# The state-space part with channels on partitions: decay and norm factors by DMA broadcast, skip and norm weights per partition

## The chip, the cores and the metric

One of the cores of a Trainium2 chip runs the whole kernel in one launch. The metric is device time in microseconds (us). TensorE (PE in the profile) multiplies matrices, PEld are its weight loads, VectorE is DVE, ScalarE ACT, GpSimd POOL, SyncE SP. All data is float32; most products are done as three products of rounded parts (hi x hi, hi x lo, lo x hi).

## What is computed

A decoder layer on 1024 positions of 1024 features: an input projection, two branches (a Conformer convolution of 31 taps and a Mamba-2 state-space branch), gates, an output projection and a gated MLP with layer norms. The change concerns the state-space branch. Cut to that (32 heads of 64 channels, 4 groups of 8 heads, state size 128, chunks of 128 positions):

```python
xbc = silu(causal_dwconv(xbc, conv_w, conv_b))          # x, B, C
dt = softplus(dt_raw + dt_bias);  a = dt * -exp(a_log)
a_cs = cumsum(a)                                        # inside a chunk
decay = where(causal, exp(a_cs[l] - a_cs[s]), 0)
y_diag = einsum(cb * decay, x * dt)                     # cb = C B^T, per chunk
states = einsum(B, exp(a_cs[-1] - a_cs), x * dt)        # carried from chunk to chunk
y_off  = einsum(C, prev_state) * exp(a_cs)
y = y_diag + y_off + x * d_skip
yg = y * silu(z);  yg = yg * rsqrt(mean(yg**2 over the 512 channels of a group) + eps)
return (yg * norm_w) @ w_out
```

## The kernel before, in words

The sequence is done in two halves of 512 positions. `mixers(hh)` holds the input projection and both branches of a half: for each of the four groups it projects the columns of B, C and the four x tiles and convolves them with 4 taps (`conv4`, L418 to L432), projects z (`z_gate`), projects two tiles of the Conformer's GLU (`glu`), and does the state-space part (`ssd_group`) in four chunks of 128 positions. The Conformer's 31 taps (`conv31`, L467) are recorded at lower priority and fill VectorE. A scheduler that models the engines' times sets the order of instructions on each engine; the order is fixed when the program is built, and each engine works through its own list. So the products of the next group's columns, z and GLU stand between the chunks of a group.

A projection is 24 products of 512 columns (L183 to L185) into one of four PSUM banks (`acc`); its weights are loaded by SyncE, copied rounded by ScalarE (L159), and the remainder is made by VectorE (L160). Small products use four other banks (`sm`).

A chunk of `ssd_group`: x tiles are transposed so that positions lie on partitions (L519), GpSimd prepares the exponents (`au`, L525), TensorE and ScalarE make the decay mask `m` (L534, L542, L543), VectorE multiplies it with C B^T (L559). Eight products of `m` with 64 columns of `xs` each give the inner part with positions on partitions and channels in columns (`py`, L581); one product of 512 columns gives the state's part (`po`, L562), scaled by VectorE with `edc` per position. VectorE adds the skip (L551), the state's part (L567) and `py` (L582) and multiplies with the chunk's z tile (L583), ScalarE squares with a row sum (L585). `normed` takes the root (L588) and reciprocal (L589) of the four chunks' sums, scales the four tiles (L591, with the norm weights as a broadcast row `nw`), and transposes them to channels on partitions for the output projection:

```python
A.activation(out=ssq, in_=ssq, func=AF.Sqrt, bias=eps, scale=1.0 / HALF)
V.reciprocal(out=ssq, in_=ssq)
for c in range(4):
    V.scalar_tensor_tensor(out=ts[c], in0=ts[c], scalar=ssq[:, c : c + 1], in1=nw, ...)
    transpose_to(yT, ts[c], c, (g % 2) * 4, 4)
```

z tiles come from a pool of five buffers (`zs`), each [128 positions, 512 channels]. Its four banks are filled side by side, and the four activations (L495) follow. The first output projection (`ssm_out_first`, weights `w_so`) reads the tiles of groups 0 and 1 in the time of group 2; the second (`w_sp`, in `combine`, L658) those of groups 2 and 3, right after the gate columns (`w_gt`, `w_gb`).

Of the kernel before, what the change touches and what calls it, by code (L numbers as in the profile page):

```python
# [8 lines left out]
F32 = mybir.dt.float32  # L9
# [36 lines left out]
RW_NW = 6 * D  # L46
RW_AL = RW_NW + 2 * D
RW_SD = RW_AL + HEADS
RW_N = RW_SD + HEADS

# [6 lines left out]
def kernel(  # L57
# [71 lines left out]
    dskip = statep.tile([P, HEADS], F32, name="dskip")  # L129
# [8 lines left out]
    edc = statep.tile([P, 3, 4, HEADS], F32, name="edc")  # L138
# [12 lines left out]
    g_scr = [dram.tile([8, P, HALF], F32, name=f"g_scr{i}") for i in range(2)]  # L151
    y_scr = [dram.tile([8, P, HALF], F32, name=f"y_scr{i}") for i in range(2)]
# [111 lines left out]
    def ln_in(hh):  # L264
        hT = big_tile(f"hT{hh}")
        with pool(f"lnin{hh}", side="right") as pl:
# [12 lines left out]
            if first:  # L279
                SY.dma_start(pc[:, :PC_N], pcol)  # L280
                SY.dma_start(a_log, prow[RW_AL : RW_AL + HEADS].partition_broadcast(P))
                SY.dma_start(dskip, prow[RW_SD : RW_SD + HEADS].partition_broadcast(P))
# [12 lines left out]
    def time_steps(pl, hh, ps):  # L295

        n2 = 2 * HEADS
        dtc = pl.tile([n2, HALF], F32, tag="yo", name=f"dtc{hh}")
# [48 lines left out]
        for c in range(4):  # L347
# [6 lines left out]
            )  # L354
        hi = pl.tile([P, HALF], F32R, tag="xsd", name=f"sp_hi{hh}")
# [18 lines left out]
        for i, m in enumerate((upper, later, ones)):  # L374
            TE.matmul(pe[:, i * n : (i + 1) * n], m, a, start=True, stop=True)
        ev = edc.rearrange("p i c h -> p (i c h)")
        A.activation(out=ev, in_=pe[:, : 3 * n], func=AF.Exp)
        V.tensor_mul(wds, dtv, edc[:, 1].rearrange("p c h -> p (c h)"))
# [99 lines left out]
    def z_gate(pl, hh, hT, g):  # L478

        pss = [bank(1) for _ in range(4)]  # L480
        for kp in range(4):
            w = weights(wz[g, kp], f"z{hh}_{g}_{kp}")
            for t in range(4):
                for k in range(2):
                    mm3(
                        pss[t],
                        lambda i: hT[:, i, 2 * kp + k, t * P : (t + 1) * P],
                        lambda i: w[:, i, k * HALF : (k + 1) * HALF],
                        kp == 0 and k == 0,
                        kp == 3 and k == 1,  # L490
                    )
        zs = []
        for t in range(4):
            z = pl.tile([P, HALF], F32, tag="zs", bufs=5, name=f"zs{hh}_{g}_{t}")
            A.activation(out=z, in_=pss[t], func=AF.Silu)  # L495
# [821 lines left out]
```

## Time and profile before

| | us |
|---|---|
| median of 3 runs (1996.41 to 1998.56) | 1997.97 |
| profiled execution | 1997.83 |
| its span | 1995.9 |
| PE busy | 1963.0 (98%) |
| DVE busy | 1688.2 (85%) |
| ACT busy | 1025.6 (51%) |
| POOL busy | 170.2 (9%) |
| granted TensorE clock, mean | 0.998 |

A group's row gives line, engine, operation, output and inputs by the program's names, shapes, the count, then the busy time in us and the mean of one in ns, then the idle time in front of it and what ended it. A row of the timeline begins with its start from the span's start and its duration, both in us; xN are N instructions in one row, the duration then from the first's start to the last's end.

### The profile page before, as it was taken

Reading aid. Unit: us, or ns where it says so; the run is one execution under the profiler, and the core shown is the slowest. Engines: PE = TensorE matmul, PEld = TensorE weight load, DVE = VectorE, ACT = ScalarE, POOL = GpSimd, SP = SyncE. Lnnn points to the kernel's source line nnn. Section 1 sums busy time; section 2 is a strip of 40 time slices with the busy share of each in tenths; the row PEclk is TensorE's granted clock in tenths of the full one; section 3 lists DMA queues with packets and bytes.
Section 4 is the critical chain, followed back from the end, with each engine's and each line's share of the span. In section 5 each row is a group of like instructions: output and inputs, shape, how many; then the busy total and the mean of one; then the engine's idle time right before and its main releaser. Section 6 shows DMA issues by size and latency. Waiting matters only on the chain. (4 is left out here: it accounts for less than half of the span.)

```text
span 1995.9 us, 24560 instructions
## 1 busy us (share of the span) xinstructions
PE 1963.0 (98%) x9140; PEld 1619.0 (81%) x9140; DVE 1688.2 (85%) x2257; ACT 1025.6 (51%) x1490; POOL 170.2 (9%) x143
## 2 busy tenths in 40 slices
PE   7999999999999999999999999999999999999997
PEld 6888887888788888888888888887878888888886
DVE  7599999989865868999998987578998888788868
ACT  5465654556453265665545546255555544553432
POOL 1010101001310000100000122001000000011000
PEclk9999999999999999999999999999999999999999
DMA  6213223333445632222323243477443232368572
GB/s 223 95 64 96 80 89 107 96 111 102 168 136 164 229 124 74 85 90 85 116 90 111 101 166 125 137 277 250 154 155 110 100 122 95 106 225 270 181 242 106
DMA packets 97032, 272.21 MB, mean 136 GB/s; under 512 B 11216, under 2 KB 11216, under 8 KB 96912
## 3 DMA queue, kind: packets, MB, share of 16 engines
q1 hardware_dynamic: 88992, 246.78, 36.8%
q0 software_dynamic: 5616, 19.66, 2.7%
q10 hardware_dynamic: 2304, 4.20, 0.6%
q8 instruction: 72, 1.18, 0.2%
q14 instruction: 48, 0.39, 0.1%
HBM read 221.05 MB, written 49.55 MB: 136 GB/s over the span
## 5 line engine op out<-in xcount | busy, mean ns | idle before, releaser
L467 DVE SCALAR_TENSOR_TENSOR c<-v,pc,c 128x512 f32<-128x512 f32 x480 | 374.5, 803 | 7.1 <-ACT c L456 5.6
L525 POOL TENSOR_TENSOR au<-seg_mv,head_of 128x1024 fp32r<-128x1024 f32 x32 | 74.8, 2336 | 958.6 <-PE sm L534 728.7
L183 PE MATMUL acc<-hT,w_c 128*128 128x512 f32 x352 | 140.9, 400 | 0.0
L184 PE MATMUL acc<-hT,w_c 128*128 128x512 f32 x352 | 140.6, 399 | 0.0
L185 PE MATMUL acc<-hT,w_c 128*128 128x512 f32 x352 | 138.5, 394 | 0.0
L956 DVE SCALAR_TENSOR_TENSOR fo<-u,pc,fo 128x1024 f32<-128x1024 f32 x88 | 111.3, 1284 | 0.4 <-ACT fo L952 0.4
L422 DVE SCALAR_TENSOR_TENSOR xbc<-u,pc,xbc 128x512 f32<-128x512 f32 x144 | 109.6, 773 | 0.5 <-ACT xbc L420 0.4
L183 PE MATMUL acc<-h1s,w_s 128*128 128x512 f32 x264 | 103.4, 392 | 2.3 <-ACT u L940 2.3
L185 PE MATMUL acc<-h1s,w_s 128*128 128x512 f32 x264 | 103.0, 390 | 0.0
L184 PE MATMUL acc<-h1s,w_s 128*128 128x512 f32 x264 | 102.8, 389 | 0.0
L184 PE MATMUL acc<-w_z,hT 128*128 128x512 f32 x256 | 100.9, 394 | 0.0
L183 PE MATMUL acc<-w_z,hT 128*128 128x512 f32 x256 | 100.7, 400 | 0.0
L185 PE MATMUL acc<-w_z,hT 128*128 128x512 f32 x256 | 100.6, 396 | 0.0
L159 ACT CAST w_c<-st_c 128x1024 fp32r<-128x1024 f32 x48 | 50.4, 1051 | 91.8 <-PE acc L185 67.5
L1095 ACT CAST w_dn<-dr 128x1024 fp32r<-128x1024 f32 (+1 forms) x73 | 60.9, 843 | 67.9 <-DVE dr L1025 35.0
L1096 DVE TENSOR_TENSOR w_dn<-dr,w_dn 128x1024 fp32r<-128x1024 f32 (+1 forms) x73 | 70.2, 967 | 14.7 <-ACT w_dn L1095 14.5
L184 PEld LDWEIGHTS acc<-hT,w_c 128*128 128x128 f32 x352 | 66.1, 188 | 16.8 <-issue 3.9
L185 PEld LDWEIGHTS acc<-hT,w_c 128*128 128x128 f32 x352 | 66.1, 188 | 16.1 <-issue 2.6
L183 PEld LDWEIGHTS acc<-hT,w_c 128*128 128x128 f32 x352 | 66.1, 188 | 15.9 <-issue 2.6
L160 DVE TENSOR_TENSOR w_c<-st_c,w_c 128x1024 fp32r<-128x1024 f32 x46 | 59.3, 1288 | 16.7 <-ACT w_c L159 16.7
L183 PE MATMUL sm<-h1b,w_s 128*128 128x512 f32 x176 | 69.1, 393 | 0.0
L184 PE MATMUL sm<-h1b,w_s 128*128 128x512 f32 x176 | 69.0, 392 | 0.0
(366 smaller groups left out, 5698.0 us busy)
## 6 DMA issues: line engine op xcount, KB each, us to landing
st_c<-wcol SPq DMA_DIRECT2D x50, 512.0 KB, 3.5
st_z<-wz SPq DMA_DIRECT2D x32, 512.0 KB, 3.4
st_wo<-wo SPq DMA_DIRECT2D x24, 512.0 KB, 4.2
ra<-wup SPq DMA_DIRECT2D x22, 512.0 KB, 3.5
rb<-wup SPq DMA_DIRECT2D x22, 512.0 KB, 3.4
t_scr<-fo POOLq DMA_DIRECT2D x22, 512.0 KB, 3.4
dr<-t_scr SPq DMA_DIRECT2D x44, 256.0 KB, 4.0
dr<-wdown SPq DMA_DIRECT2D x38, 256.0 KB, 4.3
```

The costliest lines, as they stand in the source:

```text
L159: A.copy(w[:, 0, :], st)
L160: (eng or V).tensor_tensor(out=w[:, 1, :], in0=st, in1=w[:, 0, :].bitcast(F32), op=ALU.subtract)
L183: TE.matmul(ps, wa(0), xa(0), start=start, stop=False, skip_group_check=more)
L184: TE.matmul(ps, wa(0), xa(1), start=False, stop=False, skip_group_check=more)
L185: TE.matmul(ps, wa(1), xa(0), start=False, stop=stop, skip_group_check=more)
L422: V.scalar_tensor_tensor(out=o, in0=u[:, k : k + HALF], scalar=pc[:, wc + k : wc + k + 1], in1=o, op0=ALU.mult, op1=ALU.add,)
L467: V.scalar_tensor_tensor(out=accs[i], in0=v[:, k : k + HALF], scalar=pc[:, wc + k : wc + k + 1], in1=accs[i], op0=ALU.mult, op1=ALU.add,)
L525: G.tensor_tensor(out=au, in0=seg_mv[:, c, :].unsqueeze(1).to_broadcast([P, 8, P]), in1=head_of[:, g, :].unsqueeze(2).to_broadcast([P, 8, P]),
L956: V.scalar_tensor_tensor(out=o, in0=u[:, k : k + T], scalar=pc[:, wc + k : wc + k + 1], in1=o, op0=ALU.mult, op1=ALU.add,)
L1095: A.copy(w[:, 0, cs], src)
L1096: V.tensor_tensor(out=w[:, 1, cs], in0=src, in1=w[:, 0, cs].bitcast(F32), op=ALU.subtract)
```

## The change

The state-space part leaves its result with channels on partitions.

- `z_gate` projects z like every other column, with weights as the stationary operand, so that a z tile is [128 channels, 512 positions].
- In a chunk `py` has `xs` (64 channels wide) as stationary operand and `m` as moving one, so that a head's result goes to 64 partitions, even heads to the lower, odd heads to the upper half (L577 now). The state's part is four products of 128 columns with slices of the state as the stationary operand (L563 now).
- All four chunks write into one tile `acc` [128, 4, 512]. It is preloaded with the decay factors exp(a_cs): they are made per half on ScalarE, written to memory (`e_scr`) and read back per group by two DMAs of GpSimd's queue that repeat a head's row on its 64 partitions. A chunk multiplies its part of `acc` with `po` and adds `py` (L564, L587 now).
- After the fourth chunk, tile by tile: the x tile, scaled by a weight per partition, plus `acc` (L591 now), times z (L595 now), in place in the x tile; squares on ScalarE, their sum over the four tiles on GpSimd (`ss`, L597 to L601 now).
- `normed` sums the squares over partitions with four products (`pick`, L606 now), takes root and reciprocal on [4, 128] values, writes them to memory (`r_scr`) and reads them back as a row on all partitions (L614, L615 now), both on GpSimd's queue; scales the x tiles (L618 now) and splits them with `split_to` (L203, L204 now). The 16 transposes per group are gone.
- The weights for skip and norm come as columns (`nskip`), no longer as rows.

The order of instructions changes with it. A name's first number is the half, the second the group, the third the chunk or tile; the last number only counts buffers. Order on ScalarE around the end of group 1 in the first half, before; `zs0_2` are the z tiles of group 2, `acc` their banks, `sq` the squares:

```order
L495 ACT_TABLE_LOAD
L495 ACTIVATE zs0_2_0_2433<-acc109_2313 128x512
L495 ACTIVATE zs0_2_1_2435<-acc110_2314 128x512
L495 ACTIVATE zs0_2_2_2437<-acc111_2315 128x512
L542 ACTIVATE m0_1_3_1931<-sm95_1936 128x512
L585 ACTIVATE sq0_1_2_1919,ssq0_1_1770<-t0_1_2_1892 128x512
L543 ACT_TABLE_LOAD
L543 ACTIVATE m0_1_3_1931<-m0_1_3_1931 128x512
L159 CAST w_ga0_5_2511<-st_ga0_5_2509 128x1024
L495 ACT_TABLE_LOAD
L495 ACTIVATE zs0_2_3_2439<-acc112_2316 128x512
```

And there now:

```order
L163 CAST w_gg0_5_2532<-st_gg0_5_2530 128x1024
L597 ACTIVATE ss0_1_1958<-xbc0_4_1381 128x512
L492 ACT_TABLE_LOAD
L492 ACTIVATE zs0_2_1_2367<-acc104_2337 128x512
L600 ACTIVATE sq0_1_1_1964<-xbc0_5_1421 128x512
L492 ACTIVATE zs0_2_2_2399<-acc105_2369 128x512
L600 ACTIVATE sq0_1_2_1969<-xbc0_6_1461 128x512
L492 ACTIVATE zs0_2_3_2431<-acc106_2401 128x512
```

Three of the four z activations of group 2 have moved from the middle of group 1's last chunks to behind group 1's squares; tile 0 still stands earlier. The bank of `acc104` is next used by `acc108`, the first `w_gg` product of that stretch.

VectorE at the same place, before; `c` are the Conformer's taps, `t0_1_3` the fourth chunk of group 1:

```order
L160 TENSOR_TENSOR w_gg0_5_2540<-st_gg0_5_2538,w_gg0_5_2540 128x1024
L467 SCALAR_TENSOR_TENSOR c0_2_2007<-v0_2_1696,pc_114,c0_2_2007 128x512
L467 SCALAR_TENSOR_TENSOR c0_3_2009<-v0_3_1762,pc_114,c0_3_2009 128x512
L582 TENSOR_TENSOR t0_1_3_1944<-t0_1_3_1944,sm98_1960 128x512
L467 SCALAR_TENSOR_TENSOR c0_2_2007<-v0_2_1696,pc_114,c0_2_2007 128x512
L467 SCALAR_TENSOR_TENSOR c0_3_2009<-v0_3_1762,pc_114,c0_3_2009 128x512
L583 TENSOR_TENSOR t0_1_3_1944<-t0_1_3_1944,zs0_1_3_1634 128x512
```

And there now; `xbc0_4` to `xbc0_7` are the x tiles of group 1:

```order
L587 TENSOR_TENSOR ys0_1_1770<-ys0_1_1770,sm95_1948 128x4x128
L474 SCALAR_TENSOR_TENSOR c0_2_1999<-v0_2_1698,pc_114,c0_2_1999 128x512
L474 SCALAR_TENSOR_TENSOR c0_3_2001<-v0_3_1764,pc_114,c0_3_2001 128x512
L591 SCALAR_TENSOR_TENSOR xbc0_4_1381<-xbc0_4_1381,nskip_116,ys0_1_1770 128x512
L591 SCALAR_TENSOR_TENSOR xbc0_5_1421<-xbc0_5_1421,nskip_116,ys0_1_1770 128x512
L591 SCALAR_TENSOR_TENSOR xbc0_6_1461<-xbc0_6_1461,nskip_116,ys0_1_1770 128x512
L591 SCALAR_TENSOR_TENSOR xbc0_7_1501<-xbc0_7_1501,nskip_116,ys0_1_1770 128x512
L474 SCALAR_TENSOR_TENSOR c0_2_1999<-v0_2_1698,pc_114,c0_2_1999 128x512
L474 SCALAR_TENSOR_TENSOR c0_3_2001<-v0_3_1764,pc_114,c0_3_2001 128x512
L164 TENSOR_TENSOR w_gg0_5_2532<-st_gg0_5_2530,w_gg0_5_2532 128x1024
L595 TENSOR_TENSOR xbc0_4_1381<-xbc0_4_1381,zs0_1_0_1540 128x512
```

The first multiplication with a z tile of the group has moved behind the addition of the fourth chunk, the four skips, four taps and a weight remainder. On TensorE, 11 rows (L187 to L189) stand now between the last L577 of group 1 and the first product into `acc108`; at the same place of group 0 they are 32, and in the second half 23 and 7.

VectorE at the norm of group 3 in the first half, before:

```order
L589 RECIPROCAL ssq0_3_3645<-ssq0_3_3645 128x4
L467 SCALAR_TENSOR_TENSOR c0_7_3884<-v0_7_3637,pc_114,c0_7_3884 128x512
L591 SCALAR_TENSOR_TENSOR t0_3_0_3669<-t0_3_0_3669,ssq0_3_3645,nw0_3_3643 128x512
L591 SCALAR_TENSOR_TENSOR t0_3_1_3715<-t0_3_1_3715,ssq0_3_3645,nw0_3_3643 128x512
L591 SCALAR_TENSOR_TENSOR t0_3_2_3767<-t0_3_2_3767,ssq0_3_3645,nw0_3_3643 128x512
L591 SCALAR_TENSOR_TENSOR t0_3_3_3819<-t0_3_3_3819,ssq0_3_3645,nw0_3_3643 128x512
```

And there now:

```order
L612 RECIPROCAL rr0_3_3837<-rr0_3_3837 4x128
L164 TENSOR_TENSOR w_gb0_3_4357<-st_gb0_3_4355,w_gb0_3_4357 128x1024
L618 SCALAR_TENSOR_TENSOR xbc0_12_3236<-xbc0_12_3236,nskip_116,ss0_3_3813 128x512
L618 SCALAR_TENSOR_TENSOR xbc0_13_3276<-xbc0_13_3276,nskip_116,ss0_3_3813 128x512
L618 SCALAR_TENSOR_TENSOR xbc0_14_3316<-xbc0_14_3316,nskip_116,ss0_3_3813 128x512
L618 SCALAR_TENSOR_TENSOR xbc0_15_3356<-xbc0_15_3356,nskip_116,ss0_3_3813 128x512
L204 TENSOR_TENSOR yT0_2_3036<-xbc0_12_3236,yT0_2_3036 128x512
```

One weight remainder stands between reciprocal and scaling, and the DMAs to memory and back lie between them too. On TensorE 72 rows stand between the last L577 of group 3 and its `pick`, and 7 behind it before the first `w_sp` product that reads the new tiles; in the second half likewise.

The diff, cut to its core:

```diff
+        for i in range(4):
+            ps = bank(1)
+            project(ps, weights(wz[4 * g + i], f"z{hh}_{g}_{i}"), hT)
+            z = pl.tile([P, HALF], F32, tag="zs", bufs=5, name=f"zs{hh}_{g}_{i}")
+            A.activation(out=z, in_=ps, func=AF.Silu)
...
+        eh = pl.tile([P, HALF], F32, tag="yo", bufs=2, name=f"sp_eh{hh}")
+        A.activation(out=eh, in_=pa, func=AF.Exp)
+        G.dma_start(e_scr[hh], eh)
...
-        nw = row(pl, RW_NW + g * HALF, HALF, f"nw{hh}_{g}", tag="nw")
+        acc = pl.tile([P, 4, HALF], F32, tag="ys", name=f"ys{hh}_{g}")
+        ev = e_scr[hh].rearrange("(g k i j) t -> g k j i t", k=4, j=2, i=4)
+        for j in range(2):
+            G.dma_start(acc[j * HP : (j + 1) * HP], ev[g, 0, j].partition_broadcast(HP))
...
-            V.tensor_tensor(out=heads(t), in0=heads(px), in1=per_head(dskip[:, h8]), op=ALU.mult)
...
-                TE.matmul(po, CT[:, cs], S, start=True, stop=True)
-                V.tensor_tensor(out=heads(yo), in0=heads(po), in1=per_head(edc[:, 0, c, h8]), op=ALU.mult)
-                V.tensor_add(t, t, yo)
+                for i in range(4):
+                    ts = slice(i * P, (i + 1) * P)
+                    TE.matmul(po[:, ts], S[:, ts], CT[:, cs], start=True, stop=True)
+                V.tensor_tensor(out=acc[:, :, cs], in0=by_tile(po), in1=acc[:, :, cs], op=ALU.mult)
...
-                TE.matmul(py[:, hs], m[:, h, :], xs[:, hs], start=True, stop=True)
-            V.tensor_add(t, t, py)
-            V.tensor_mul(t, t, zs[c])
-            A.activation(out=sq, in_=t, func=AF.Square, accum_out=ssq[:, c : c + 1])
+                TE.matmul(
+                    py[h % 2 * HP : (h % 2 + 1) * HP, h // 2 * P : (h // 2 + 1) * P],
+                    xs[:, h * HP : (h + 1) * HP], m[:, h, :], start=True, stop=True)
+            if first:
+                A.copy(acc[:, :, cs], by_tile(py))
+            else:
+                V.tensor_tensor(out=acc[:, :, cs], in0=acc[:, :, cs], in1=by_tile(py), op=ALU.add)
+        for i, y in enumerate(xT):
+            V.scalar_tensor_tensor(out=y, in0=y, scalar=nskip[:, 1, k : k + 1], in1=acc[:, i, :],
+                op0=ALU.mult, op1=ALU.add)
+            V.tensor_mul(y, y, zs[i])
+            A.activation(out=sq, in_=y, func=AF.Square)
+            G.tensor_add(ss, ss, sq)
...
+            for c in range(4):
+                TE.matmul(pm[:4, :P], pick[:, c, :], ss[:, c * P : (c + 1) * P], start=c == 0, stop=c == 3)
+            A.activation(out=r, in_=pm[:4, :P], func=AF.Sqrt, bias=eps[:4], scale=1.0 / HALF)
+            V.reciprocal(out=r, in_=r)
+            G.dma_start(rd.rearrange("(c t) -> c t", c=4), r)
+            G.dma_start(ss, rd.partition_broadcast(P))
+            for i, y in enumerate(xT):
-                transpose_to(yT, ts[c], c, (g % 2) * 4, 4)
+                V.scalar_tensor_tensor(out=y, in0=y, scalar=nskip[:, 0, k : k + 1], in1=ss,
+                    op0=ALU.mult, op1=ALU.mult)
+                split_to(yT, (g % 2) * 4 + i, y)
```

More of the change, by code (lines that the diff above doesn't have):

```diff
@@ L297, in time_steps @@
         n2 = 2 * HEADS
[L298 removed]
+        dtc = pl.tile([n2, HALF], F32, tag="yo", bufs=2, name=f"dtc{hh}")
         A.activation(
@@ L587, in normed @@
         def normed(yT):
-            A.activation(out=ssq, in_=ssq, func=AF.Sqrt, bias=eps, scale=1.0 / HALF)
-            V.reciprocal(out=ssq, in_=ssq)
+            pm = bank(0)
             for c in range(4):
+                TE.matmul(
+                    pm[:4, :P], pick[:, c, :], ss[:, c * P : (c + 1) * P],
+                    start=c == 0, stop=c == 3,
+                )
+            r = pl.tile([4, P], F32, tag="rr", name=f"rr{hh}_{g}")
+            A.activation(out=r, in_=pm[:4, :P], func=AF.Sqrt, bias=eps[:4], scale=1.0 / HALF)
```

80 lines of the change are left out of this document (39 added, 41 removed).

## The prediction

> **What bounds the kernel now.** I read the page's first part, then the waits of TensorE, then the windows by stage, and last the groups and the timeline around the places that the change touches.
>
> ```profile
> span 1995.9 us, 24560 instructions
> ## 1 busy us (share of the span) xinstructions
> PE 1963.0 (98%) x9140; PEld 1619.0 (81%) x9140; DVE 1688.2 (85%) x2257; ACT 1025.6 (51%) x1490; POOL 170.2 (9%) x143
> ...
> PE sm L209 <- DVE x L260: 13.3, 2, 12.1
> ...
> PE acc L184 <- DVE yT L216: 1.5, 1, 1.5
> ...
> PE acc L183 <- ACT gb L644: 0.6, 1, 0.6
> ```
>
> TensorE is busy in 98% of the span, and its waits (total, times, longest) are the start (13.3 us, before the first transposes) and little else: the two waits for the state-space output in front of `w_sp` are 1.5 and 0.6 us. So a microsecond of TensorE work that goes is a microsecond gained, and any wait of TensorE that the change adds is a microsecond lost. In the state-space stretches VectorE is just as full:
>
> ```profile
> 100.00:300.00 200.00, 200.00 (x965) 164.09 (x964) 199.78 (x274) 125.32 (x203) 18.63 (x8) 1.00 0.25 82
> ...
> 780.00:1000.00 220.00, 220.00 (x1062) 180.40 (x1061) 219.46 (x304) 130.37 (x198) 20.75 (x9) 1.00 0.28 90
> ```
>
> The columns are length, PE, PEld, DVE, ACT, POOL. VectorE works 199.78 of 200 us there, because the Conformer taps (L467) fill every hole; it always has something queued ahead of what TensorE will want next.
>
> **The change, TensorE work.** L203, L204, L382, L492, L563, L577, L587, L595, L606 and L618 are lines of the changed kernel, all others of the kernel before. A row's duration overlaps with the next one, so I cost by the step from start to start.
>
> ```profile
> 299.62 0.39 PE L185 MATMUL acc<-yT,w_so 128*128 128x512 f32 x1
> ...
> 300.30 0.39 PE L185 MATMUL acc<-yT,w_so 128*128 128x512 f32 x1
> ...
> 278.57 1.89 PE L581 MATMUL sm<-xs,m 128*128 128x64 f32 x16
> ...
> 516.36 1.91 PE L209 MATMUL sm<-ident,t 128*128 128x128 f32 x16
> ...
> L581 PE MATMUL sm<-xs,m 128*128 128x64 f32 x512 | 60.5, 271 | 0.0
> ...
> L209 PE MATMUL sm<-ident,t 128*128 128x128 f32 x128 | 15.3, 273 | 0.0
> ...
> 30.27 0.62 PE L394 MATMUL acc<-hT,w_c 128*64 128x256 f32 x4
> 30.72 1.24 PE L404 MATMUL acc<-hT,w_c 128*128 128x256 f32 x9
> 31.80 0.63 PE L394 MATMUL acc<-hT,w_c 128*64 128x256 f32 x4
> 32.26 0.40 PE L404 MATMUL acc<-hT,w_c 128*128 128x256 f32 x2
> 32.50 0.63 PE L394 MATMUL acc<-hT,w_c 128*64 128x256 f32 x4
> ```
>
> Between the two L185 rows lie three steps: 0.68 / 3 = 0.227 us for 512 columns. L581 steps by (1.89 - 0.27) / 15 = 0.108, L209 by (1.91 - 0.27) / 15 = 0.109, though one moves 64 columns and the other 128: here the 128-column weight load sets the step, not the columns. L394, whose weights are 64 columns wide, steps by 0.45 / 4 = 0.113 for 256 columns. A float32 product leaves two rows (L581 has 512 rows for 256 products).
> - Within a chunk (L577 now): 512 rows of 128 columns with 64-wide weights. Scaled from L394, 128 columns are 0.056; I take 0.060, since the 0.120 that L404 shows for the same 256 columns with 128-wide weights leaves a few ns for a load. 512 x (0.060 - 0.108) = -24.6 us. Bounds: 0.108, no gain at all; 0.030, half of my value, if two half-width products ran at once.
> - The 128 transposes of `normed` go: 128 x 0.109 = -14.0 us.
> - The state's share (L563): one product of 512 columns (2 x 0.227 = 0.45) becomes four of 128, eight rows at the load's 0.109 = 0.87. 28 chunks have it: +11.8 us.
> - The four `pick` products per group: 64 rows at 0.060 (0.030 to 0.109): +3.8 us. One product fewer per half at L382: -0.4 us. The z projection has the same 768 rows at 0.227 as before, only with the operands swapped: 0.
>
> Sum: -23.4 us. At the pattern of weight widths a rule speaks against this. The rows above go from 128-wide to 64-wide weights and back four times, and 4 x 0.113 and 9 x 0.120 fill the starts from 30.27 to 31.80 exactly, so the switch costs nothing that shows. The Trainium skill (TensorEngine Tiling (Array Packing), Key Properties) says that a change of tiling mode drains the TensorEngine; were each of the 80 switches an empty pipe of one row (0.27 us), the total would rise by an estimated 22 us, to about 2043 us. By the rows I take nothing for it.
>
> **The change, waits for z.** Before, a chunk used its own z tile and gave it back (the product with `zs[c]`, L583). Now all four z tiles of a group are held until the whole group is summed, since they lie by channel. There are five buffers. z projections of the next group run between the chunks, so their first tile takes the fifth buffer and the second must wait for the multiplication of `zs[0]` at the group's end; until then its product stays in its PSUM bank, and the fourth `acc` product after it (`w_gg`) needs that bank. In the order, `w_gg` follows the last L577 of a group after 32 rows (group 0, first half), 11 (group 1, first half), 23 (group 0, second half) and 7 (group 1, second half), which at 0.227 is a cover of 7.3, 2.5, 5.2 and 1.6 us. In groups 2 and 3 no z of a next group is due there. What must happen in that time:
>
> ```profile
> 278.69 2.07 DVE L467 SCALAR_TENSOR_TENSOR c<-v,pc,c 128x512 f32<-128x512 f32 x3
> 280.68 1.21 DVE L160 TENSOR_TENSOR w_gg<-st_gg,w_gg 128x1024 fp32r<-128x1024 f32 x1
> 281.81 1.41 DVE L467 SCALAR_TENSOR_TENSOR c<-v,pc,c 128x512 f32<-128x512 f32 x2
> 283.14 0.68 DVE L582 TENSOR_TENSOR t<-t,sm 128x512 f32<-128x512 f32 x1
> 283.74 1.41 DVE L467 SCALAR_TENSOR_TENSOR c<-v,pc,c 128x512 f32<-128x512 f32 x2
> ...
> L585 ACT ACTIVATE sq<-t 128x512 f32<-128x512 f32 x32 | 20.2, 631 | 19.7 <-DVE t L583 19.7
> L495 ACT ACTIVATE zs<-acc 128x512 f32<-128x512 f32 x32 | 18.4, 598 | 7.0 <-PE acc L185 6.9
> ...
> L495 ACT ACT_TABLE_LOAD x7 | 9.0, 1283 | 0.1
> ```
>
> The last product of group 1 ended at 278.57 + 1.89 = 280.46, and VectorE read it at 283.14, because of what stood ahead in its order: a lag of 2.7 us, which TensorE did not feel. VectorE steps 0.60 for an addition (283.14 to 283.74), 0.66 for a tap or a scalar_tensor_tensor (three in 2.0), 1.13 for a weight remainder. The new order from L587 to the first L595: addition 0.60, two taps 1.3, the four skips 2.6, two taps 1.3, a remainder 1.1, the multiplication 0.7: 7.7 us. Then ScalarE: the square 0.63, a table load 1.28, the z activation 0.60, and some 0.1 for the semaphores. With the lag 13.0 us. The wait of TensorE:
> - group 1, first half: 13.0 - 2.5 = 10.5;
> - group 0, first half, where no table load stands between: 11.7 - 7.3 = 4.4;
> - group 0, second half, without the remainder: 11.8 - 5.2 = 6.6;
> - group 1, second half: 13.0 - 1.6 = 11.4.
>
> Together 32.9 us. I take the one measured lag; without any it is 22.1, with twice that lag 43.7.
>
> **The change, the norm's round trip.** Behind group 3 the first `w_sp` product needs the normalised tiles. Before, this was a square root, a reciprocal, four scalings and transposes, and TensorE waited 1.5 and 0.6 us. Now the factors go to memory and come back as a broadcast.
>
> ```profile
> L685 POOL TENSOR_TENSOR var<-var,csq 128x512 f32<-128x512 f32 x14 | 22.6, 1612 | 14.4 <-ACT csq L684 13.5
> ...
> L589 DVE RECIPROCAL ssq<-ssq 128x4 f32<-128x4 f32 x8 | 1.3, 168 | 1.0 <-ACT ssq L588 1.0
> ...
> L588 ACT ACTIVATE ssq<-ssq,eps 128x4 f32<-128x4 f32 x8 | 2.4, 298 | 0.1
> ...
> g_scr<-gt SPq DMA_DIRECT2D x16, 256.0 KB, 2.0
> ...
> nw<-prow SPq DMA_DIRECT2D x8, 256.0 KB, 3.3
> ```
>
> Three GpSimd additions of 1.6 us feed `pick`; 72 rows (16.3 us) cover them: lag 2.7, VectorE to the second product with z 5.9, square 0.6, additions 4.8, sum 14.0. From `pick` on: root 0.3, reciprocal 0.2, store 2.0 (nearest row g_scr, a bigger one), the broadcast 3.3 (nw was the same 2 KB row to 128 partitions), four scalings in a row on VectorE 2.6, the first remainder 0.7, hops 0.5: 9.6 us. Behind `pick` stand 7 rows (1.6 us) that do not need it. Wait 8.0, twice 16.0, less the 2.1 of before: +13.9 us. Bounds for the two transfers: 4 to 8 us together, so 11 to 19. In the same wait VectorE stands with nothing queued that TensorE wants sooner, and on GpSimd the Conformer mean (L672 before) queues behind the second transfer; its product is due 16 us further on in TensorE's order. After groups 0, 1 and 2 the same round trip is covered: the order puts five to six us of taps between reciprocal and scaling, and the first product that reads the result is over 10 us off. The decay factors' loads (1 MB a group through GpSimd's queue, held by VectorE's skips) have from the group's end to the next chunk, at least 15 us; I take 0. The eight row loads of norm weights that leave SyncE's queue were waited for by nobody: 0.
>
> **Sum.** The profiled execution took 1997.8 us, with 1.9 us around its span and 0.1 us below the median of the runs (1998.0): 1997.8 - 23.4 + 32.9 + 13.9 = 2021.2 us. A measurement of this kernel can tell 0.2% from no change, so this is slower.
>
> **The rivals.**
> - *VectorE paces the stretch*: 1978 us. Then TensorE's new waits fall where VectorE would have held it anyway, and the time goes with VectorE's work:
>
> ```profile
> L551 DVE TENSOR_TENSOR t<-sm,dskip 128x512 f32<-128x512 f32 x32 | 21.6, 675 | 0.0
> ...
> L567 DVE TENSOR_TENSOR t<-t,yo 128x512 f32<-128x512 f32 x28 | 19.0, 678 | 0.0
> ...
> L591 DVE SCALAR_TENSOR_TENSOR t<-t,ssq,nw 128x512 f32<-128x512 f32 x32 | 21.8, 741 | 0.0
> ```
>
>   L551 and L567 go (-40.6), 32 skips come (32 x 0.741 = +23.7), four additions move to ScalarE (-2.7): -19.6. For it: 199.78 of 200 us busy. Against it: TensorE is full in the same 200 us and the waits name VectorE with 1.5 us. It decides if TensorE's waits on VectorE fill less than the 23 us saved. Chance 0.12.
> - *Half-width products run side by side*: L577 at 0.030, another -15.4: 2006 us. No row here shows two at once, L394's step fits one after the other. The Trainium skill (TensorEngine Tiling (Array Packing), Key Properties) says that different tiles can load weights and multiply in parallel; no run here shows it yet. Chance 0.09.
> - *Half-width products keep the old step*, 0.108, by the load or by a drain at each switch: +24.6, 2046 us. For it: no row has a float32 product this narrow; against it, L394 steps by its columns. Chance 0.08.
>
> **How the numbers follow.** My forecast has 0.71, predicted time 2021 us, its own range 2003 to 2040 from the lag (22.1 to 43.7) and the transfers (11 to 19). The range to hold 8 in 10 takes in both slower rivals and leaves out the first: 1998 to 2046. Slower by over 0.2% (above 2002): 0.68 of the forecast, 0.05 of the second rival, all of the third: 0.81. Faster (below 1994): 0.12. Within: 0.07.
>
> **What would show it.** L577 in steps of 0.06 (right), 0.11 or 0.03 (rivals). In TensorE's waits, `w_gg` on the activation L492 four times, 4 to 11 us each, and `w_sp` on L203 or L204 twice, 8 us each. If these waits are absent and VectorE is full, the first rival is right; if TensorE waits elsewhere for longer, above all for GpSimd's au or the decay loads, my list of places was short.

## The result, and the profile after

The changed kernel takes 2045.78 us (median of 4 runs, 2044.87 to 2048.25) against 1997.19 us beside it: ratio 1.0247, interval 1.0230 to 1.0265. It is 49 us slower; the forecast was slower by 23.

First the page of the changed kernel, with the span and the busy time of each engine:

```profile
span 2046.4 us, 24805 instructions
...
PE 1956.4 (96%) x9240; PEld 1600.1 (78%) x9240; DVE 1712.2 (84%) x2230; ACT 1020.2 (50%) x1458; POOL 237.0 (12%) x201
```

The span grew by 50.5 us. TensorE works 6.6 us less than before (1963.0), so the time in which it does not work grew by 57.1. VectorE, with 27 instructions fewer, is busy for 24.0 us more (before 1688.2); the prediction, where it priced VectorE for its first rival, had it at 19.6 less. GpSimd has 66.8 us more.

TensorE's waits in the changed kernel (total, times, longest):

```profile
PE acc L187 <- ACT zs L492: 36.4, 4, 12.6
PE acc L187 <- ACT yT L203: 16.3, 2, 8.4
...
PE sm L567 <- ACT bt L557: 5.0, 4, 2.4
...
PE acc L188 <- DVE yT L204: 2.3, 2, 1.1
PE sm L606 <- POOL ss L601: 2.1, 1, 2.1
```

The first line is the z wait, at the four places that were named, the second and fourth the norm in front of `w_sp`. Two were not on the list: a chunk's product waits for ScalarE's copy of B, and `pick` for GpSimd's sum. TensorE's timeline at the four z waits; the bracket is the wait in front of the row:

```profile
184.35 0.79 PE L187 MATMUL acc<-hT,w_gg 128*128 128x512 f32 x1 [4.57 <-ACT zs L492]
...
293.45 0.80 PE L187 MATMUL acc<-hT,w_gg 128*128 128x512 f32 x1 [11.21 <-ACT zs L492]
294.04 0.63 PE L188 MATMUL acc<-hT,w_gg 128*128 128x512 f32 x1
294.47 0.63 PE L189 MATMUL acc<-hT,w_gg 128*128 128x512 f32 x1
...
874.56 0.80 PE L187 MATMUL acc<-hT,w_gg 128*128 128x512 f32 x1 [8.05 <-ACT zs L492]
...
985.33 0.80 PE L187 MATMUL acc<-hT,w_gg 128*128 128x512 f32 x1 [12.59 <-ACT zs L492]
```

Forecast were 4.4, 10.5, 6.6 and 11.4. The two rows without a bracket step by 0.43 where these products step by 0.227 elsewhere. The windows around that wait show why; after the busy times comes the granted clock:

```profile
272.00:282.00 10.00, 10.00 (x54) 7.53 (x52) 10.00 (x15) 1.05 (x1) 0.00 (x0) 1.00 0.16 52
282.00:293.00 11.00, 0.23 (x2) 0.00 (x0) 11.00 (x17) 3.16 (x4) 1.27 (x2) 0.70 0.46 116
293.00:296.00 3.00, 2.55 (x6) 2.07 (x7) 3.00 (x6) 2.40 (x5) 2.01 (x1) 0.50 1.01 259
```

The clock falls during the wait (0.70) and is 0.50 in the 3 us behind it; before, it was 1.00 throughout these stretches. The Trainium skill (TensorE: Matmul & The Clock Gate, Part 1) says that an idle window of some 3.4 us halves the clock; by the rows here the trace agrees. And VectorE works in all 11 us of the wait.

The chunk's `py` and the `pick` products of the changed kernel:

```profile
278.11 0.39 PE L187 MATMUL acc<-hT,w_ga 128*128 128x512 f32 x1
278.43 1.09 PE L577 MATMUL sm<-m,xs 128*64 128x128 f32 x16
279.45 0.50 PE L188 MATMUL acc<-hT,w_ga 128*128 128x512 f32 x1
279.79 0.40 PE L189 MATMUL acc<-hT,w_ga 128*128 128x512 f32 x1
...
303.85 1.04 PE L606 MATMUL sm<-ss,pick 128*4 128x128 f32 x8 [2.08 <-POOL ss L601]
```

A row of `py` steps by (1.09 - 0.27) / 15 = 0.055: forecast 0.060. A `pick` row, as narrow or narrower, takes (1.04 - 0.27) / 7 = 0.110. A whole block costs more than its rows, for the projection's rows around it, which step by 0.23, step by more there. So I account for a block from its start to the second projection row behind it, less 0.23 for the first one, and add what the step in front is longer than 0.23. For `py` that is 279.79 - 278.43 - 0.23 = 1.13, and 0.09 in front: 1.22 us per chunk, of which 16 rows are 0.88. The other 0.34 lie at the changes from 128-wide to 64-wide weights and back. In the kernel before the block L581 cost 280.58 - 278.57 - 0.23 = 1.78 us, and the step in front was the usual 0.23.

The state's part, one product of 512 columns before and four of 128 now:

```profile
223.73 1.02 PE L562 MATMUL sm<-state,xbc 128*128 128x512 f32 x2
224.19 0.79 PE L183 MATMUL acc<-hT,w_c 128*128 128x512 f32 x1
224.82 0.40 PE L184 MATMUL acc<-hT,w_c 128*128 128x512 f32 x1
```

```profile
228.13 1.05 PE L563 MATMUL sm<-xbc,state 128*128 128x128 f32 x8
228.94 0.48 PE L189 MATMUL acc<-hT,w_c 128*128 128x512 f32 x1
229.25 0.40 PE L187 MATMUL acc<-hT,w_c 128*128 128x512 f32 x1
```

By the same account they cost 0.86 and 0.89 us: nearly the same, where the forecast had 0.45 and 0.87.

### The profile page after: what moved, and what is told of

The parts are those of the page before. It is cut to its first block, busy times and chain, and to the rows that moved or that the text cites. A ratio compares the mean times of both kernels' runs of the same rounds, so it can differ in the third digit from the quotient of the medians.

```text
span 2046.4 us, 24805 instructions
## 1 busy us (share of the span) xinstructions
PE 1956.4 (96%) x9240; PEld 1600.1 (78%) x9240; DVE 1712.2 (84%) x2230; ACT 1020.2 (50%) x1458; POOL 237.0 (12%) x201
## 4 chain that ended last, share of the span: by engine, by line
PE 57%; DVE 31%; issue 5%; DMA 4%; ACT 2%; SPq 0%; DVEq 0%; POOLq 0%; ACTq 0%
PE acc L189 15%; PE acc L188 15%; PE acc L187 15%; DVE c L474 12%; PE sm L187 3%; PE sm L189 3%; PE sm L188 3%; DVE xbc L429 2%; DMA ss<-r_scr 1%; PE acc L411 1%; DVE m L558 1%; DVE w_c L164 1%; DVE xs L548 1%; DVE w_z L164 1%; DVE xbc L591 1%
## 5 line engine op out<-in xcount | busy, mean ns | idle before, releaser
L474 DVE SCALAR_TENSOR_TENSOR c<-v,pc,c 128x512 f32<-128x512 f32 x480 | 390.7, 839 | 6.0 <-ACT c L463 3.8
L189 PE MATMUL acc<-hT,w_c 128*128 128x512 f32 x352 | 139.1, 395 | 0.0
L187 PE MATMUL acc<-hT,w_c 128*128 128x512 f32 x352 | 138.9, 395 | 0.0
L187 PE MATMUL acc<-h1s,w_s 128*128 128x512 f32 x264 | 103.3, 391 | 2.3 <-ACT u L968 2.3
L189 PE MATMUL acc<-h1s,w_s 128*128 128x512 f32 x264 | 103.0, 390 | 0.0
L188 PE MATMUL acc<-hT,w_z 128*128 128x512 f32 x256 | 101.0, 394 | 0.0
L187 PE MATMUL acc<-hT,w_z 128*128 128x512 f32 x256 | 100.8, 394 | 0.0
L189 PE MATMUL acc<-hT,w_z 128*128 128x512 f32 x256 | 100.3, 392 | 0.0
L187 PE MATMUL acc<-hT,w_gg 128*128 128x512 f32 x128 | 53.7, 419 | 36.4 <-ACT zs L492 36.4
L189 PEld LDWEIGHTS acc<-hT,w_c 128*128 128x128 f32 x352 | 66.1, 188 | 16.1 <-issue 2.5
L187 PEld LDWEIGHTS acc<-hT,w_c 128*128 128x128 f32 x352 | 66.1, 188 | 14.7 <-issue 1.4
L187 PE MATMUL sm<-h1b,w_s 128*128 128x512 f32 x176 | 69.1, 393 | 0.0
```

Of the source, the lines that this page charges most:

```text
L187: TE.matmul(ps, wa(0), xa(0), start=start, stop=False, skip_group_check=more)
L188: TE.matmul(ps, wa(0), xa(1), start=False, stop=False, skip_group_check=more)
L189: TE.matmul(ps, wa(1), xa(0), start=False, stop=stop, skip_group_check=more)
L474: V.scalar_tensor_tensor(out=accs[i], in0=v[:, k : k + HALF], scalar=pc[:, wc + k : wc + k + 1], in1=accs[i], op0=ALU.mult, op1=ALU.add,)
```

## The experiments

All ratios are to the kernel before, run on the same chip, with intervals of about 0.0015 to either side; a difference between two of them is uncertain by some 0.002, or 4 us. 0.001 is 2.0 us. In e6, e10 and e13 to e16 the kernel leaves something out and does not compute the layer.

| run | ratio |
|---|---|
| changed kernel | 1.0247 |
| e1 heads of one half in a row | 1.0287 |
| e2 seven z buffers | 1.0150 |
| e3 last norm factors spread by products | 1.0204 |
| e4 products in front of `w_sp`; e7 in front of all six long waits | 1.0253; 1.0251 |
| e5 = e2 and e3 | 1.0107 |
| e5 with: e6 no skips; e8 norm recorded later; e9 sums on VectorE | 1.0091; 1.0142; 1.0101 |
| e11 z columns behind GLU's, and e3; e12 with VectorE's sums too | 1.0082; 1.0079 |
| e17 = e11, all norm factors spread by products | 1.0111 |
| e5 without: e13 scaling; e14 all but scaling; e10 the whole norm | 0.9981; 0.9898; 0.9832 |
| e15 = e14 with the squares and their sums | 0.9956 |
| e16 kernel before without its norm | 0.9966 |

**The z waits (e2, e11).** e2, which to make room also gives the tiles tagged `yo` and `ya` one buffer instead of two (so do all runs built on it):

```diff
-z = pl.tile([P, HALF], F32, tag="zs", bufs=5, name=f"zs{hh}_{g}_{i}")
+z = pl.tile([P, HALF], F32, tag="zs", bufs=7, name=f"zs{hh}_{g}_{i}")
```

> Seven z buffers in place of five (yo and ya get one buffer each, to make room). Theory A, the four z waits and the low clock behind them cost what the trace shows: the 36.4 us of w_gg waits go, and with them some 8 us of half-speed products behind them: 1998 to 2006 us. Theory B, VectorE paces these stretches (it was busy in every microsecond of the four waits): the waits come back at other places of TensorE, above all in front of the chunk products and w_sp, and the time stays above 2025 us.

Measured 1.0150, 19 us less than the changed kernel, between the two. TensorE's waits in this run:

```profile
PE acc L187 <- ACT yT L203: 18.0, 3, 8.9
...
PE sm L577 <- DVE m L558: 8.0, 2, 4.8
PE sm L606 <- POOL ss L601: 6.8, 2, 5.3
```

The z waits are gone, and 36.4 us of wait were worth 19: 12.7 us came back as waits for the mask product (new) and the squares' sum (from 2.1). In e11 the order of the projections changes instead, on top of e3:

```diff
+vs = [(i, glu(pl, hh, hT, i)) for i in (2 * g, 2 * g + 1)]
 zs = z_gate(pl, hh, hT, g)
-vs = [(i, glu(pl, hh, hT, i)) for i in (2 * g, 2 * g + 1)]
```

> Five z buffers as in the changed kernel, but the z columns of a group are projected behind its GLU columns, so that the banks of the waiting z tiles are next needed over 100 products later; with the last norm factors spread by products. Theory A, the z waits are a matter of buffers alone and either remedy is worth the same: ratio 1.009 to 1.012. Theory B, the single yo and ya buffers that made room for seven z tiles cost something themselves (squares that wait for GpSimd's sum): ratio 1.008 or below. If the order of the columns matters by itself, above 1.014.

Measured 1.0082, at the border between the two; against e5 (1.0107) 5 us, hardly more than the uncertainty. It and e12 are the fastest of the runs that have the new layout and compute the whole layer, and still slower than the kernel before.

**The last norm (e3, e5).**

```diff
+rb = ss
+if g < 3:
     rd = r_scr[hh][g]
     G.dma_start(rd.rearrange("(c t) -> c t", c=4), r)
     G.dma_start(ss, rd.partition_broadcast(P))
+else:
+    rb = bank(0)
+    for c in range(4):
+        TE.matmul(rb[:, c * P : (c + 1) * P], ident[:4, c : c + 1].to_broadcast([4, P]), r,
+                  start=True, stop=True)
...
-        out=y, in0=y, scalar=nskip[:, 0, k : k + 1], in1=ss,
+        out=y, in0=y, scalar=nskip[:, 0, k : k + 1], in1=rb,
```

> For the last group of each half only, the norm factors are spread over the partitions by four products with a column of the identity (4 rows stationary) into a PSUM bank, instead of going to memory and back. Theory A, the store (2.2 us) and the load (4.1 us) with their hops are on the path in front of w_sp: its wait falls from 8.4 and 8.0 us to about 3.5 each, and too little idle time is left for the clock to halve behind it (3.5 and 3.0 us saved): 2046 - 10 - 6 = about 2030 us. Theory B, something else is nearly as late there (a weight cast, the gate's table load, VectorE): less than 5 us saved, 2041 us or more.

Measured 1.0204, 9 us less, between the two. The two `w_sp` waits, 18.6 us together, became 7.8:

```profile
PE acc L188 <- DVE yT L204: 4.8, 2, 2.5
...
PE acc L187 <- ACT yT L203: 3.0, 2, 1.5
```

So the two transfers were on the path. e5 is e2 and e3 together.

> The seven z buffers and the spreading of the last norm factors by products, together. Theory A, the two losses are separate: the ratio to before falls from 1.0150 (seven buffers alone) by the 0.0043 that the spreading gave alone, to 1.0107, about 2016 us. Theory B, VectorE holds the rest: the norm's wait comes back behind VectorE's steps and the ratio stays at 1.013 or above.

Measured 1.0107, theory A: the two losses add up, and 21 us remain.

**The half clock (e4, e7).** e4, in `combine`:

```diff
 gate(1)
+pf = bank(0)
+for _ in range(32):
+    TE.matmul(pf, hT[:, 0, 0, :P], hT[:, 0, 0, :], start=True, stop=True)
```

> 32 products of 512 columns whose result nobody reads stand on TensorE between the pick products and the w_sp product that waits for the norm, in both halves. They do not shorten the path. Theory A, the low clock behind the wait is paid on top of the wait: with TensorE kept busy the products behind run at full speed, 3.6 and 3.0 us are saved, 2039 us. Theory B, the low clock costs nothing of its own (the time is given back by what waits later anyway): 2046 us; if the 7.3 us of products add to the path, 2060 us.

Windows of e4 at the first `w_sp` wait and behind it:

```profile
533.00:541.00 8.00, 7.37 (x32) 5.57 (x30) 2.59 (x4) 1.72 (x3) 1.09 (x2) 1.00 0.15 50
541.00:549.00 8.00, 6.59 (x27) 5.10 (x28) 4.93 (x7) 5.52 (x8) 0.00 (x0) 1.00 0.42 139
```

and the same windows of the changed kernel:

```profile
533.00:541.00 8.00, 0.00 (x1) 0.00 (x1) 2.68 (x4) 1.32 (x3) 1.08 (x2) 0.65 0.32 118
541.00:549.00 8.00, 6.85 (x15) 5.07 (x16) 3.69 (x6) 5.67 (x8) 0.78 (x1) 0.50 0.33 100
```

The clock stays at 1.00, and 27 products are done in the second window instead of 15. Yet the kernel's time is the same, 1.0253: theory B. e7 fills the z waits as well: the projection of `w_ga` ends with 16, 44, 30 or 50 products by a tile of zeros.

> The changed kernel with products by a tile of zeros in front of all six long waits: 16, 44, 30 and 50 behind the w_ga columns whose w_gg waits for z, 32 in front of each w_sp. They fill 3.6, 10.0, 6.8 and 11.3 us of the z waits and 7.3 us of each norm wait, and remove no wait. Theory A, the half clock behind the waits is a loss of its own: no stretch with granted clock 0.50 is left, and 8 to 12 us go: 2034 to 2038 us. Theory B, what TensorE gains there it loses at the next wait for VectorE: 2043 to 2048 us.

Measured 1.0251: no gain, theory B. The mean granted clock rose from 0.984 to 0.995, so not every stretch at half clock is gone. The page of e7:

```profile
PE 1996.5 (98%) x9444; PEld 1631.5 (80%) x9444; DVE 1707.2 (83%) x2231; ACT 1023.0 (50%) x1460; POOL 241.6 (12%) x201
```

The 204 added products are 204 x 0.227 = 46.3 us. Without them TensorE works 1950.2 us, 6 less than in the changed kernel, and the rest of the span (2046.6 us) is 6 us longer. What full speed saves behind a wait is waited for at a later place: TensorE's wait for the squares' sum, for one, is 5.6 us instead of 2.1.

**Two halves at once (e1).**

```diff
-for h in range(8):
+for h in (0, 2, 4, 6, 1, 3, 5, 7):
```

> The eight heads of a chunk are multiplied in the order 0, 2, 4, 6, 1, 3, 5, 7, so that neighbouring products go to the same half of the PSUM partitions, save one pair. Theory A, two half-width products run at once only when they go to different halves: a product then steps by about 0.218 us as the pick products do (two rows of 0.109), instead of 0.109; 7 of 8 products per chunk lose about 0.1 us each, 32 chunks: +20 to +26 us, 2066 to 2072 us. Theory B, the step of 0.054 per row is that of one narrow product alone: the rows keep their step, 2046 us.

Measured 1.0287, 8 us more. A chunk's `py` in e1:

```profile
279.92 1.58 PE L577 MATMUL sm<-m,xs 128*64 128x128 f32 x16
```

1.58 us instead of 1.09 for the same 16 rows: products to different halves overlap, products to the same half hardly do. That is theory A, with a smaller size: 0.49 x 32 = 16 us, since the heads around the change of half still overlap, and TensorE's z waits are 6.5 us shorter for it (29.9 us instead of 36.4). The Trainium skill's rule that different tiles can multiply in parallel (TensorEngine Tiling (Array Packing), Key Properties) agrees with this run.

**What else could remain (e6, e8, e9, e12, e17).** Five attempts at the 21 us of e5. e6:

```diff
-V.scalar_tensor_tensor(out=y, in0=y, scalar=nskip[:, 1, k : k + 1], in1=acc[:, i, :],
-                       op0=ALU.mult, op1=ALU.add)
-V.tensor_mul(y, y, zs[i])
+V.tensor_mul(y, acc[:, i, :], zs[i])
```

> As the run with both remedies, and the skip term is left out: acc times z without the x tile, so that VectorE has 32 steps of 0.66 us fewer, four in a row (2.65 us) at each group's end. Theory A, with the z waits gone it is VectorE's burst at the group's end that holds TensorE (chunk products behind the mask product L558, the pick product behind the squares): 5 to 15 us faster than with the skips. Theory B, VectorE has room there and the burst is covered: within 3 us of the run with the skips.

Measured 1.0091, 3 us: theory B, though VectorE is busy for 12.0 us less (1691.5). e8 records `done(yT)` of groups 0 to 2 just ahead of the next group's `ssd_group`.

> As the run with both remedies, but the norm of groups 0, 1 and 2 is recorded behind the next group's z and GLU projections, so that pick, root, scalings and remainders come later in each engine's order. Theory A, these 5 us of VectorE work per group and the early pick product (6.8 us of waits for the squares) hold TensorE at the group ends: 5 to 10 us faster than without. Theory B, VectorE is short of time in the whole stretch, so that moving the work only moves the wait: within 3 us.

Measured 1.0142, 7 us slower than e5; neither theory had that. e9 sums the squares of groups 1 and 3 on VectorE:

```diff
+if g % 2:
+    V.tensor_add(acc[:, 0:2], acc[:, 0:2], acc[:, 2:4])
+    V.tensor_add(ss, acc[:, 0], acc[:, 1])
```

> As the run with both remedies (ratio 1.0107), but in groups 1 and 3 the squares go into the free slices of acc and are summed by VectorE (1.2 and 0.6 us) instead of GpSimd. Theory A, GpSimd's sum, of which one addition took 6.6 us beside a busy VectorE and the next 1.3 us beside an idle one, is what the pick product waits for: the 6.8 us of waits for the squares' sum go, and 5 to 8 us with them: ratio 1.007 to 1.008. Theory B, the additions lengthen VectorE's own list by as much and the wait moves: within 3 us, 1.009 or above.

Measured 1.0101, no difference from e5, though VectorE is busy for 5.6 us less (1697.9 instead of 1703.5). e12 does the same on e11.

> As the run with the z columns behind the GLU's and the last norm factors spread by products, and with the squares of groups 1 and 3 summed by VectorE. Theory A, the three remedies are separate: 5 to 8 us below the run without VectorE's sums. Theory B, VectorE's list only gets longer: within 3 us. If both z and norm waits were all that made the kernel slower, this one ends at or below the kernel before, ratio 1.000 or less.

Measured 1.0079: no difference again, with VectorE busy for 5.8 us less (1697.0 instead of 1702.8). e17 spreads the factors of all groups by products.

> As the run with the z columns behind the GLU's (ratio 1.0082), but the norm factors of all groups, not only of the last, are spread by products, so that no transfer of factors is left in GpSimd's list; TensorE gets 24 products more, 6 x 0.9 = 5 us. Theory A, the transfers of groups 0, 1 and 2 are covered: 1 to 6 us slower, ratio 1.009 to 1.011. Theory B, they hold VectorE's scalings and GpSimd's next exponents up: 5 us faster or more, ratio 1.006 or below.

Measured 1.0111, 6 us slower than e11: the transfers of groups 0, 1 and 2 are covered, as the prediction said, and the added products are paid.

**The norm as a whole (e10, e16, e13, e14, e15).** In e10 only `split_to` is left of `normed`, and the squares and `ss` are gone.

> As the run with both remedies, with the norm left out: no squares, no sums, no factors, no scaling; the x tiles are split as they are. Theory A, what is left of the loss (some 21 us) is the norm's work and waits: TensorE's work alone then decides, 1962.7 less 17.7 less 7.7 for the pick products, with 17 us of waits: about 1985 us, ratio 0.995 or below. Theory B, it is the rest of the group's end, the four skips and four multiplications with z behind the last chunk: ratio 1.003 or above.

Measured 0.9832: 55 us less than e5. That is theory A and more than it expected; but the terms that it names add up to 1954 us, not to its 1985, and 1962 were measured. The page of e10:

```profile
PE 1928.7 (99%) x9176; PEld 1585.5 (81%) x9176; DVE 1655.3 (85%) x2190; ACT 985.1 (50%) x1408; POOL 183.2 (9%) x161
```

TensorE works 34 us less than in the kernel before, and behind the start its longest wait group, 2.3 us for the tile `u`, was there before as well. The control is e16; of its `normed` only the transposes are left.

> The kernel before with its norm left out (no squares, no root, no reciprocal, no scaling; the 128 transposes stay). Theory A, the norm of before is hidden, since TensorE waits there for 2.1 us only: within 6 us of the kernel before, ratio 0.997 to 1.000, so that the norm's 55 us are a cost of the new form alone. Theory B, VectorE's time counts in both kernels alike: 20 us or more, ratio 0.990 or below.

Measured 0.9966 (0.9954 to 0.9978), next to theory A: there the norm costs 7 us, in the new form, measured on e5, 55. Three runs divide the 55. e13 is e5 without the scaling (L618 of the changed kernel), so that nothing waits for the factors any more. The edit of e15:

```diff
 A.activation(out=sq, in_=y, func=AF.Square)
 G.tensor_add(ss, ss, sq)
-pm = bank(0)
...
+rb = ones[:, :1].to_broadcast([P, HALF])
```

The scaling multiplies by the ones `rb`. e14 has the same edit, and the two upper lines are gone too.

> As the run with both remedies (ratio 1.0107), with sums, pick, root, reciprocal and transfers as they are, but the factors are not used: the x tiles are split unscaled, so that 32 steps of VectorE (25.8 us) and the wait for the factors go. Theory A, VectorE's time is what the norm costs: some 25 us less, ratio 0.998 or below. Theory B, it is the chain that the engines' lists hold (pick behind the sums, root and reciprocal in front of the next group's mask): at most the last groups' waits go, 5 to 8 us, ratio 1.006 or above.

> As the run with both remedies, with the scaling kept (by a column of ones) and all that makes the factors left out: squares, sums, pick, root, reciprocal, transfers and spreading. Theory A (VectorE's scalings cost it): only TensorE's 11 us for pick and spreading and the last groups' waits of 7 us go, ratio 1.001 to 1.003. Theory B (the chain, GpSimd's sums included): most of the 55 us go, ratio 0.990 or below.

> As the run with the scaling alone, but with the squares on ScalarE and the 24 additions on GpSimd kept, whose result nobody reads. Theory A, GpSimd's additions hold VectorE up (three taps beside a GpSimd product took 3.8 us instead of 2.0) and so the whole stretch: 10 to 25 us above the run with the scaling alone. Theory B, they lie beside VectorE's work: within 4 us of it, and the chain behind the sums is what costs.

Measured 0.9981, 0.9898 and 0.9956: e13 at the border of its theory A, e14 its theory B, e15 its theory A. From e10 upward: the scaling 13 us (e14), the squares and sums 12 (e15), and pick, root, reciprocal, transfers and spreading 30 (e5). Taken out of the whole, the scaling is worth 25 (e13), so the parts are not independent: each is dearer where the others stand. The pages of e14 and of e15:

```profile
PE 1933.6 (98%) x9176; PEld 1587.9 (80%) x9176; DVE 1680.9 (85%) x2222; ACT 981.8 (50%) x1404; POOL 181.6 (9%) x161
```

```profile
PE 1939.7 (98%) x9176; PEld 1588.1 (80%) x9176; DVE 1703.8 (86%) x2222; ACT 1018.7 (51%) x1452; POOL 227.5 (11%) x185
```

VectorE has 2222 instructions in both, and is busy for 22.9 us more in e15, which has the squares on ScalarE and the 24 additions on GpSimd. Half of it lies in the 32 scalings, in e14 and in e15:

```profile
L600 DVE SCALAR_TENSOR_TENSOR xbc<-xbc,nskip,ones 128x512 f32<-128x512 f32 x32 | 22.0, 737 | 0.0
```

```profile
L607 DVE SCALAR_TENSOR_TENSOR xbc<-xbc,nskip,ones 128x512 f32<-128x512 f32 x32 | 34.1, 1087 | 0.0
```

In e15, 19 of them overlap an instruction of GpSimd and take 1.33 us on average, the other 13 take 0.74; in e14 none overlaps one. One place of e5 shows it closely, VectorE's timeline first, then GpSimd's:

```profile
975.61 3.79 DVE L474 SCALAR_TENSOR_TENSOR c<-v,pc,c 128x512 f32<-128x512 f32 x3
```

```profile
975.64 1.90 POOL L526 TENSOR_TENSOR au<-seg_mv,head_of 128x1024 fp32r<-128x1024 f32 x1 [0.47 <-PE sm L535]
```

Three taps, 2.07 us in the row that the prediction shows, take 3.79 while GpSimd works for 1.90. The Trainium skill (SBUF — State Buffer, Who interferes with whom) says that VectorE and GpSimd share a pair of ports under an exclusive lock; the trace agrees, the difference of 1.7 us being about GpSimd's own time. Over the whole kernel, the taps in the kernel before, and in the changed one:

```profile
L467 DVE SCALAR_TENSOR_TENSOR c<-v,pc,c 128x512 f32<-128x512 f32 x480 | 374.5, 803 | 7.1 <-ACT c L456 5.6
```

```profile
L474 DVE SCALAR_TENSOR_TENSOR c<-v,pc,c 128x512 f32<-128x512 f32 x480 | 390.7, 839 | 6.0 <-ACT c L463 3.8
```

The same 480 taps take 16.2 us more; the reciprocal (L612 now), on 4 partitions with 128 values each instead of 128 with 4, takes 934 ns instead of 168.

The page also follows the work that ended last back through the engines. Its shares of the span in the changed kernel, and in e10:

```profile
PE 57%; DVE 31%; issue 5%; DMA 4%; ACT 2%; SPq 0%; DVEq 0%; POOLq 0%; ACTq 0%
```

```profile
PE 90%; DVE 6%; DMA 2%; issue 1%; ACT 1%; SPq 0%; DVEq 0%; ACTq 0%
```

So VectorE lies on the chain for 31% of the span in the new layout, and hardly without the norm. The share does not measure the loss: it is 22% in e5, and 24% in e14, which is 42 us faster.

## Why the prediction was wrong

Sign and places were right, the size was half. The 2046 us of the last rival are met by chance: its step of 0.108 is not there. By the runs, in us:

| term | forecast | from runs |
|---|---|---|
| TensorE work without `pick` | -27.2 | -26.8, with all else but norm and z waits (e16 to e10: 0.9966 to 0.9832) |
| z waits | +32.9 | +19.4 (changed kernel to e2) |
| last norm | +13.9, the whole wait | +8.6, its transfers (e2 to e5) |
| rest of the norm | +3.8 (`pick`) | +48.1 (e10 to e5, 54.9, less the 6.8 of e16) |
| sum | +23.4 | +49.3 |

The right column goes from run to run, from the kernel before to the changed one, and so adds up by itself; where the parts depend on each other, another order would divide it otherwise.

- *TensorE work* is right in its sum, by luck, and is there to be had: without a norm in either kernel the new layout is 27 us faster. In the changed kernel it is covered up. By the rows, `py` gives (1.22 - 1.78) x 32 chunks = -17.9 us, forecast -24.6; the state's part +0.03 x 28 = +0.8, forecast +11.8, because I took a float32 product of 512 columns for two rows of 0.227, the step of the rounded parts, and it costs 0.86; `pick` costs 305.15 less 303.85 less 0.23 = 1.07 per group, 8.6 in all, forecast 3.8. With the transposes and L382 as forecast that is -22.9 for -23.4: three errors that nearly cancel.
- *The step of 0.060* was right for a wrong reason: I scaled it from `w_c` rows, but a `pick` row with as many columns takes 0.110. The products are fast because two of them overlap; the rival that said so was right in its mechanism, and its 0.030 was half of a wrong figure. The change between narrow and wide weights, for which I took nothing, costs 0.34 us per chunk, 11 in all, half of the 22 that I had worked out for a drain; no run tells whether a drain is what it is.
- *The z waits* were sized well (36.4 for 32.9) and priced badly: I took each microsecond of wait as lost. VectorE works through them, so that taking them away gave 19 us, and waits for the mask and the sums took their place.
- *The norm* is the step that failed: the sum had nothing for it behind groups 0, 1 and 2 but `pick`'s work. "After groups 0, 1 and 2 the same round trip is covered" is true of the transfers (e17), and I let it stand for the whole norm; the wait in front of `w_sp` I had at 16.0 us for 18.6 measured. The norm also has steps in the lists of ScalarE, VectorE and GpSimd at every group, and with `pick` these cost 48 us more than in the old form. Before, its sums came out of the squares' own instruction on ScalarE, and the whole norm cost 7 us.
- *VectorE* was mis-counted with it. In the rival I counted instructions, 19.6 us less, and gave GpSimd's additions no part in VectorE's time. It got 24.0 us more. The rival that VectorE paces the stretch had its mechanism half right (scalings taken away are worth 25 us, e13), with the opposite sign, since VectorE's time grew.
- *The list of places was short* by B's copy and the sum in front of `pick`, 7.1 us in the changed kernel.
- *The half clock* was missing from the sum, and as far as e4 and e7 remove it, it is no term of it.
- *The range* of the forecast, 2003 to 2040, does not follow from the two bounds named for it, which give 2007 to 2037.

What stays open is which of the norm's steps cost the 48 us, and how. That GpSimd's additions lengthen VectorE's work is shown (e14, e15). That this makes the kernel slower is likely from e15, 12 us slower than e14, but e15 also has the squares, and e9 and e12 speak against it: there VectorE makes 12 of the 24 additions, is busy for 5.6 and 5.8 us less, and the time stays. So a microsecond of VectorE has no one price: 32 steps are worth 25 us as scalings (e13, where the wait for the factors goes too), 13 when all that makes the factors is gone (e14), and 3 as skips (e6). Of the 30 us between e15 and e5 the profiled executions have 25: TensorE is busy for 16.3 more, some 9 of them `pick` and spreading (80 rows of 0.110), and idle for 8.9 more. The mean granted clock is 0.997 in e15 and 0.990 in e5, so that half clock may be a part of the rest; products in the waits were tried on the changed kernel alone.

## What to carry to other kernels

Where TensorE and VectorE are both full, price a wait by what is waited for next when it is gone, not by its length. Count work moved to a third engine in the busy time of the second as well, for GpSimd's 24 additions lengthened VectorE's by 22.9 us, where VectorE would have made them in some 24 x 0.60 = 14; whether that is lost time only a run tells, since taking half of them back changed nothing (e9, e12). A reduction that came free with another instruction (the row sum of the squares) is dear once the layout puts it across partitions: count all its steps in every engine's list, at every group, not only where TensorE is seen to wait. Price a row from rows of the same type, not of the same shape. Leave a whole step out of both kernels, old and new, to see what each form of it costs.

## What the runs showed of the hardware

- Float32 products with 64-wide weights to different halves of the output partitions step by 0.055 us per row of 128 columns; with neighbours in the same half a chunk takes 1.58 us instead of 1.09. A block of 16 such rows among 128-wide ones costs 1.22 us, 0.34 more than its rows.
- With 128-wide weights a float32 product of 512 columns costs 0.86 us and four of 128 columns 0.89, while a row of 512 columns of the rounded parts steps by 0.227.
- Behind a wait of 8 us the granted clock is 0.50 for about 8 us; with products in the wait it stays at 1.00, and the kernel's time does not change (1.0253 and 1.0251 against 1.0247).
- 24 GpSimd additions of 128 x 512, with their squares on ScalarE, add 22.9 us to VectorE's busy time at the same number of instructions; a scaling that overlaps GpSimd takes 1.33 us, one that does not 0.74.
